# Two-layer attention and convolution encoder: four depthwise taps per layer taken out of the last two wide sections, and the last head's copy, addition and division put in another order

## The chip, the core and the metric

The kernel runs on one core of a Trainium2 chip. A core has five engines, each with its own queue of instructions that it works off in order: TensorE (PE; matrix products, into PSUM), VectorE (DVE), ScalarE (ACT), GpSimd (POOL) and SyncE (SP; it only issues transfers here). GpSimd issues transfers too. The metric is the time of one execution on the device in microseconds, lower is better.

## The reference

One sequence of 1024 positions with 1024 channels goes through two layers. Cut to the half of a layer that the change touches:

```python
h = rmsnorm(x, g_mix[l]);  p = h @ w_in[l]              # 1024 x (384 + 256 + 32 + 1024)
c_q  = rmsnorm(p[:, :384], g_q[l]);   q  = c_q @ w_uq[l]      # 8 heads x (64 + 32 rotary)
c_kv = rmsnorm(p[:, 384:640], g_kv[l]); kv = c_kv @ w_ukv[l]  # 8 heads x (64 key + 64 value)
y_attn = softmax(q k^T / sqrt(96)) v                          # per head, blocks of 128 queries
a, gt = split(p[:, 672:]);  u = a * sigmoid(gt)               # 512 channels
u = silu(layernorm(dwconv(u, w_dw_conv[l], taps=31)))         # depthwise, along the sequence
x = x + concat(y_attn, u) @ w_o[l]
x = x + gated_conv_ffn(rmsnorm(x))                            # up, 3 taps, silu gate, down
```

All is float32. The depthwise convolution is a sum of 31 taps: `conv[c, t] += w[c, tap] * u[c, t + tap - 15]`.

## The kernel before

Channels lie on the partitions, positions along the rows; a block is a tile of 128 x 1024. Each matrix product is made of three, from high and low parts of both sides (names ending in h and l), so that the result is as exact as in float32. A layer is `project` (the products with w_in, w_uq, w_ukv), `attention` and `feed` (w_o and the ConvFFN).

**`project`** walks through a list of sections. A wide section (a0 to a3, g2, g3, kv0, kv1, q0, q1, q2) multiplies the 1024 channels of h by one tile of 128 columns of w_in; the planner counts 10.9 us for it. Behind the wide sections come four short ones for the keys (k0 to k3, 2.72 us each) and six for the queries (u0, u1, n0 to n3, 4.08 us each). A section accumulates into one PSUM tile of 128 x 1024, of which `project` has three, used in turn: u0 takes the tile of k1, u1 that of k2, n0 that of k3. A key section's tile comes free in `key` (L727 to L735): ScalarE copies it into the high part kh (L733, called `kh<-pk` in the trace), then VectorE subtracts kh from it for the low part kl (L735).

The weights come by `supply` (L861), which goes by the planner's clock. GpSimd issues a transfer of the tile into its high part (`cast_tile`, L171). Later (`complete`) ScalarE writes the negative of the high part into the low part (L175) and GpSimd issues a transfer that adds the source onto it (L176). There are eight tiles for these parts; the tiles of wu1 (the weights of n2, n3 and of the rotary part) come free when section q2, the last wide one, is done with wq2.

**The 31 taps** of the depthwise convolution are done for four groups of 128 channels, into the tiles conv_0 to conv_3, in several ways, and none takes TensorE:
- near taps: one VectorE instruction each (`conv_step`, L1790), placed by the planner in `project`;
- far taps (`tap_far`, L1793 to L1797): ScalarE multiplies the group by the tap's weight into a tile (L1796), and GpSimd issues a transfer that adds the tile to conv (L1797). They are chosen in the loop over the sections (L885 to L890): in each wide section at most `FAR_TOGETHER` = 3, of the groups whose near taps are done, one per group, from the list `away[j]` of taps that the group has left;
- late taps: what is left in `away[j]` when `project` is done. `attention` spreads them over its steps (L1711 to L1723). Most are done by `tap_late` on GpSimd (L1802: multiply; L1808: a transfer adds the product to conv). In layer 0, the first 13 that group 0 has left are instead multiplied by VectorE at the steps of `STEP_AT` and added by GpSimd's own instruction (L1806) one step later. In layer 1 there are none of that kind.

**`attention`** goes through steps n = −2 to 64: eight heads with eight tiles of 128 queries each. In step n TensorE transposes the probabilities of tile n (`pt`, copied out of PSUM by ScalarE at L1615 or VectorE at L1616) and computes the scores of tile n + 2 (`s`), ScalarE takes the exponential (`p`, L1600), and in odd steps `values` (L1621) multiplies probabilities and values into a PSUM tile o (L1639). A table `agenda[n]` holds work to be recorded at the end of step n. In it stand, among others, the late taps, the first weights of w_o (transfers of four tiles at step 50, L916; their low parts, L175, from step 55 on) and the sums for the layernorm.

When half of a head (512 queries) is done, `gather` (L1649) copies one of the two halves of o with ScalarE (L1653, `yt<-o`) and adds the other with VectorE (L1654), which frees the PSUM bank. For the last head, the sums of the exponentials are inverted (`inverse`, L1682, `rc`), brought onto all partitions by TensorE (`spread`, L1685, at L301 in the trace, `rc_71s`: it takes a PSUM bank that the addition has freed), and `divide` (L1688) multiplies; `early` (L1691) begins the products with w_o in the attention's last steps and `early_add` (L1696) adds them to the residual.

Of the kernel before, what the change touches and what calls it, by code (L numbers as in the profile page):

```python
# [74 lines left out]
KEY_AT = (4.0, -8.6)  # L75
NEAR_ORDER = (0, 1, 2, 3)
FAR_TOGETHER = 3
FAR_GAP = 8.0
NPAR = P_BF + 2 * NF
HALVES = (slice(0, 512), slice(512, T))  # L80
# [39 lines left out]
class Encoder:  # L120
# [456 lines left out]
    def project(self, l, carry):  # L577
        nc, a = self.nc, self.a
        par = self.par[l]
        clock = {"pe": 0.0, "dve": 0.0}  # L580
        taps, active, u, conv, away, far_at = [], [], {}, {}, {}, {}
# [6 lines left out]
        st = {}  # L588

        def work(until):  # L590
            while True:
                at = next((e for e in active if e[0] <= clock["dve"]), None)
                if at is None and taps and clock["dve"] + TAP <= until:
                    j, t = taps.pop(0)
                    self.conv_step(l, j, u[j], conv[j], t)
                    clock["dve"] += TAP
                    continue
                if at is None:
                    at = min(active, key=lambda e: e[0], default=None)
                    if at is None or at[0] > until:  # L600
                        return
                    clock["dve"] = max(clock["dve"], at[0])
                step = next(at[1], None)
                if step is None:
                    active.remove(at)
                else:
                    clock["dve"] += step[0]
                    at[0] = clock["dve"] + step[1]

        def launch(steps, n=-1):  # L610
            active.append([clock["pe"], steps, n])

        def finish(n):
            for e in [e for e in active if e[2] <= n]:
                for step in e[1]:
                    clock["dve"] = max(clock["dve"], e[0]) + step[0]
                    e[0] = clock["dve"] + step[1]
                active.remove(e)
# [210 lines left out]
        add = lambda name, weight, emit, evict, after=None: seq.append((name, weight, emit, evict, after))  # L829
# [24 lines left out]
        times, starts, t = {}, {}, 0.0  # L854
# [6 lines left out]
        def supply(now, turn=TURN):  # L861
            while coming and coming[0][1] <= now + LEAD:
                name, at = coming.pop(0)
                turning.append((name, at, self.cast(l, name)))
            while turning and turning[0][1] <= now + turn:
                name, at, e = turning.pop(0)
                w[name] = self.complete(*e)
# [10 lines left out]
        for n, (name, weight, emit, evict, after) in enumerate(seq):  # L878
            supply(clock["pe"])
            finish(n - 3)  # L880
            ps[name] = self.wide(f"p{name}{l}")
            emit()
            clock["pe"] += times[name]
            queue = [i for i, _ in taps]
            far = [j for j in away if clock["pe"] >= far_at[j] and  # L885
                   (j not in queue or queue.count(j) == NEAR_TAPS[l][j] and queue.index(j) > 8)]
            work(clock["pe"] - times[name] / 2)
            for j in sorted(far, key=far_at.get)[:FAR_TOGETHER if times[name] > 5.0 else 0]:
                self.tap_far(l, j, away[j].pop(0), u[j], conv[j])
                far_at[j] = clock["pe"] + FAR_GAP  # L890
            work(clock["pe"])
            if after:
                after()
            launch(evict(), n)
# [665 lines left out]
    def attention(self, l, u, conv, away, spill, keys, kvs, loaded, ahead, wo, begun):  # L1560
        nc = self.nc
# [3 lines left out]
        state, v = {}, []  # L1565
# [55 lines left out]
        def values(pair, n):  # L1621
            h, qp = divmod(pair, 4)
            st = state[h]
            e = h % 2
            gg = qp // 2
            main, aux = slice(e * 64, e * 64 + 64), slice(64 - e * 64, 128 - e * 64)
            if qp % 2 == 0:
                if gg == 0 and e == 0:
                    st["y"], st["rb"] = self.blk(f"yt{l}_{h}"), self.blk(f"rb{l}_{h}")
                elif gg == 0:  # L1630
                    st["y"], st["rb"] = state[h - 1]["y"], state[h - 1]["rb"]
                st["po"] = self.bank(f"o{l}_{h}_{gg}")
            po = st["po"]
            cs = slice(qp % 2 * 256, qp % 2 * 256 + 256)
            for g in range(2):
                pt = st["pt"].pop((qp, g)).rearrange("p k q r t -> p k (q r t)")
                for i in range(4):
                    k = 4 * g + i
                    nc.tensor.matmul(po[ROW_TILES[i % 2], cs], v[k // 2][:, k % 2, h * 64:h * 64 + 64], pt[:, i, :],  # L1639
                                     start=k < 2, stop=k > 5)  # L1640
            if qp % 2 == 0:
                return
            if n >= total:
                gather(h, gg, main, aux, n)
            else:
                m = n + (h == last)
                agenda[m].append(lambda: gather(h, gg, main, aux, m))

        def gather(h, gg, main, aux, n):  # L1649
            st = state[h]  # L1650
            y, rb, po = st["y"], st["rb"], st["po"]
            qs = HALVES[gg]
            nc.scalar.copy(out=y[main, qs], in_=po[aux, :])  # L1653
            nc.vector.tensor_tensor(out=y[main, qs], in0=po[main, :], in1=y[main, qs], op=ALU.add)  # L1654
            if h < HEADS - 2:
                if gg:
                    agenda[n + 1].append(lambda: turned(h, main, rb, y))
            elif n > total:
                divide(y[main, qs], main, h, gg)
            else:  # L1660
                agenda[n + 1].append(lambda: divide(y[main, qs], main, h, gg))
                if h == last:
                    agenda[n + 1].append(lambda: finish(last, y, 0))
# [4 lines left out]
        def turned(h, main, rb, y):  # L1668
            pr = self.bank(f"sr{l}_{h}", (64, 128))
            nc.tensor.transpose(pr, self.inverse_sums, self.ident)  # L1670
            rs = self.cp.tile([8, 128], F32, name=f"rs{l}_{h}", tag="rs", bufs=2)
            nc.vector.tensor_copy(out=rs, in_=pr[0:8, :])
            nc.sync.dma_start(out=sd[h].rearrange("(a b) -> a b", a=8), in_=rs)
            nc.sync.dma_start(out=rb[main, :], in_=sd[h:h + 1].partition_broadcast(64))
            if h % 2:
                agenda[h * 8 + 10 + Y_DELAY].append(lambda: nc.gpsimd.tensor_tensor(out=y, in0=y, in1=rb, op=ALU.mult))
                agenda[h * 8 + 10 + Y_DELAY + (Y_DELAY if h < 5 else Y_LAST)].append(
                    lambda: ys.append(self.split(y, f"ys{l}_{h}", on_pool=True)))
# [9 lines left out]
        def divide(ym, main, h, c):  # L1688
            nc.vector.tensor_tensor(out=ym, in0=inv.pop((h, c))[main, :], in1=ym, op=ALU.mult)
# [10 lines left out]
        def finish(h, y, c):  # L1700
            cs = HALVES[c]
            if c == 0:
                ys.append([self.blk(f"ys{l}_{h}{i}", F32R) for i in "hl"])
            hi, lo = (t[:, cs] for t in ys[-1])
            nc.scalar.copy(out=hi, in_=y[:, cs])
            nc.vector.scalar_tensor_tensor(out=lo, in0=y[:, cs], scalar=1.0, in1=hi.bitcast(F32), op0=ALU.mult, op1=ALU.subtract)

        ys, inv, po = [], {}, begun["po"]
        total = HEADS * 8
        agenda = defaultdict(list)  # L1710
# [4 lines left out]
        for i, (_, j, t) in enumerate(late):  # L1715
            n = LATE_FROM + int((SIDE_TIME - LATE_FROM) * sum(costs[:i]) / sum(costs))
            if kinds[i] == "step":
                m, tap = STEP_AT[l][stepped.index(i)], self.tap_late(l, j, t, u[j], conv[j], nc.vector)
# [8 lines left out]
        last = HEADS - 1  # L1727
# [11 lines left out]
        for n in range(-2, total + 1):  # L1739
            if n % 2 and n > 2:  # L1740
                values((n - 3) // 2, n)
# [8 lines left out]
            if n + 2 < total:  # L1750
                h, qt = divmod(n + 2, 8)
# [18 lines left out]
            if n == total:  # L1770
                early(1, range(3))
                values(2 * total // 4 - 1, total + 1)
# [178 lines left out]
```

## Time and profile before

| | |
|---|---|
| time, median of 3 runs | 2251.78 us (2249.91 to 2252.26) |
| the profiled execution's own time | 2249.61 us |
| its span (first to last instruction in the trace) | 2247.8 us |
| TensorE busy | 2220.4 us, 99% |
| VectorE busy | 1674.3 us, 74% |
| ScalarE busy | 1242.0 us, 55% |
| GpSimd busy | 677.4 us, 30% |
| mean granted clock of TensorE | 0.996 |

A row of a timeline reads: start in us, duration in us, engine, line of the kernel, operation, output<-inputs, shapes, count (xN), and in brackets how long the engine stood idle ahead of it and what released it. Consecutive instructions of one kind are drawn together in one row with their count; a row's start is the first one's. Layer 0's sections run to about 200 us, its attention to about 400 us; layer 1's sections run to about 1316 us and its attention to about 1520 us.

### The profile page before, as it was taken

The page shows a single profiled execution, that of the slowest core. Times are in us where ns is not written, and L with a number is a line of the kernel's source. Part 1 is how long each engine was busy: PE and PEld are TensorE (multiplying, and loading weights), DVE is VectorE, ACT ScalarE, POOL GpSimd, SP SyncE. Part 2 cuts the span into 40 slices and gives each one's busy share as a digit, 9 for nine tenths or more (in the row PEclk, how much of TensorE's full clock was granted, in tenths as well). Part 3 has the DMA queues.
Part 4 walks back from the last instruction along what each step waited for, and adds up shares of the span by engine and source line. Part 5 has one row for each costly group of instructions (what it writes and reads, how often), then busy time and mean ns, then how long its engine had stood idle before and what let it go on. Part 6 is the DMA issues. An engine that isn't in the chain of part 4 may idle for free.

```text
span 2247.8 us, 34428 instructions
## 1 busy us (share of the span) xinstructions
PE 2220.4 (99%) x12750; PEld 1781.9 (79%) x12750; DVE 1674.3 (74%) x2220; ACT 1242.0 (55%) x1896; POOL 677.4 (30%) x782
## 2 busy tenths in 40 slices
PE   9999999999999999999999899999999999999998
PEld 7887666888888888888878776668888888888887
DVE  7987877668777776876579777776797777768765
ACT  5454777447555555544523557774475555555444
POOL 1232676232333332002412224542323333320032
PEclk9999999999999999999999999999999999999999
DMA  6899998766899998935958999876669999988356
GB/s 186 166 187 276 196 199 174 195 170 128 227 275 299 272 303 207 330 109 143 210 130 168 186 271 211 189 166 178 159 155 233 297 288 278 294 211 297 101 130 166
DMA packets 196921, 469.65 MB, mean 209 GB/s; under 512 B 24113, under 2 KB 32017, under 8 KB 196753
## 3 DMA queue, kind: packets, MB, share of 16 engines
q0 software_dynamic: 97904, 217.45, 48.0%
q1 hardware_dynamic: 98272, 248.96, 33.2%
q8 instruction: 100, 1.64, 0.3%
q10 hardware_dynamic: 576, 1.05, 0.1%
q14 instruction: 69, 0.56, 0.1%
HBM read 305.35 MB, written 80.40 MB: 172 GB/s over the span
## 4 chain that ended last, share of the span: by engine, by line
PE 83%; DVE 6%; DMA 5%; issue 4%; ACT 1%; POOL 1%; POOLq 0%; ACTq 0%; SPq 0%; DVEq 0%
PE p L1144 33%; PE pd L1332 17%; PE po L955 7%; PE s L1590 6%; PE o L1639 5%; PE pa L212 3%; PE t L1613 3%; PE pg L212 2%; PE pg L574 2%; PE pn L212 1%; DMA conv<-far 1%; DVE conv L1790 1%; PE pv L1574 1%; PE pu L212 1%; PE pa L574 1%
## 5 line engine op out<-in xcount | busy, mean ns | idle before, releaser
L1144 PE MATMUL p<-b,w 128*128 128x512 f32 x3552 | 807.4, 389 | 0.3
L1144 PEld LDWEIGHTS p<-b,w 128*128 128x128 f32 x3552 | 666.0, 188 | 141.0 <-DVE w L1526 1.3
L1332 PE MATMUL pd<-ab,wd 128*128 128x512 f32 (+1 forms) x1920 | 422.3, 381 | 0.0
L1332 PEld LDWEIGHTS pd<-ab,wd 128*128 128x128 f32 x1920 | 350.8, 188 | 69.5 <-DVE ab L1526 0.4
L176 POOL DMA_DIRECT2D w<-wu x96 | 84.3, 881 | 357.5 <-ACT w L175 323.9
L1592 DVE TENSOR_REDUCE mx<-s 128x1 f32<-128x1024 f32 x128 | 156.3, 1221 | 34.9 <-PE s L1590 31.4
L1600 ACT ACTIVATE p<-s,mx 128x1024 f32<-128x1024 f32 x128 | 142.9, 1117 | 55.0 <-DVE mx L1592 52.2
L1538 DVE SCALAR_TENSOR_TENSOR o<-zg,par,o 128x1023 f32<-128x1023 f32 x88 | 112.8, 1284 | 76.3 <-ACT o L1532 75.0
L1790 DVE SCALAR_TENSOR_TENSOR conv<-gate,par,conv 128x1023 f32<-128x1023 f32 (+14 forms) x127 | 161.6, 1275 | 4.5 <-ACT conv L636 1.5
L176 POOL DMA_DIRECT2D w<-in_w_up x116 | 100.4, 866 | 200.6 <-ACT w L175 174.5
L175 ACT ACTIVATE w<-w 128x512 fp32r<-128x512 f32 x212 | 133.5, 630 | 3.0
L1524 ACT CAST ab<-ac 128x512 fp32r<-128x512 f32 x130 | 80.1, 617 | 97.6 <-DVE ac L1267 94.9
L1093 DVE TENSOR_TENSOR zg<-p,zg 128x512 f32<-128x512 f32 x88 | 60.6, 690 | 98.3 <-PE p L1144 91.6
L1639 PE MATMUL o<-pt,v 128*64 128x256 f32 x1024 | 126.9, 386 | 1.7 <-DVE pt L1616 1.1
L1616 DVE COPY pt<-t 128x512 f32<-128x512 f32 x128 | 87.8, 686 | 52.6 <-PE t L1613 51.9
L916 POOL DMA_DIRECT2D wd<-in_w_down x44 | 32.6, 744 | 308.7 <-PE pd L1332 307.9
L1538 DVE SCALAR_TENSOR_TENSOR v<-zv,par,v 128x1023 f32<-128x1023 f32 x88 | 112.5, 1281 | 10.5 <-ACT v L1532 10.4
L1524 ACT CAST w<-wu 128x512 fp32r<-128x512 f32 x84 | 51.8, 619 | 123.5 <-DVE wu L1093 121.5
L1111 ACT CAST w<-wu 128x512 fp32r<-128x512 f32 x96 | 58.9, 614 | 92.7 <-DVE wu L1093 89.0
L1639 PEld LDWEIGHTS o<-pt,v 128*64 128x64 f32 x1024 | 67.7, 136 | 52.1 <-issue 18.9
L1613 PEld LDWEIGHTS t<-ident,p 64*128 64x128 f32 x2048 | 76.8, 138 | 38.3 <-issue 27.0
L1526 DVE TENSOR_TENSOR ab<-ac,ab 128x512 fp32r<-128x512 f32 x130 | 89.4, 690 | 21.2 <-ACT ab L1524 14.1
(2123 smaller groups left out, 4315.1 us busy)
## 6 DMA issues: line engine op xcount, KB each, us to landing
w<-in_w_up POOLq DMA_DIRECT2D x232, 256.0 KB, 7.4
wu<-in_w_up SPq DMA_DIRECT2D x88, 512.0 KB, 5.2
w<-wu POOLq DMA_DIRECT2D x96, 256.0 KB, 5.8
sd<-in_w_down SPq DMA_DIRECT2D x44, 512.0 KB, 9.1
ws<-sd SPq DMA_DIRECT2D x44, 512.0 KB, 8.1
wd<-in_w_down POOLq DMA_DIRECT2D x88, 256.0 KB, 5.3
act<-v SPq DMA_DIRECT2D x36, 512.0 KB, 5.7
ac<-act SPq DMA_DIRECT2D x72, 256.0 KB, 5.8
```

Source lines behind the costliest of these rows:

```text
L176: self.nc.gpsimd.dma_start(out=lo, in_=src, accum_op=ALU.add)
L212: nc.tensor.matmul(ps[:, HALVES[c]], w, x[:, HALVES[c]], start=(k == 0 and s == 0), stop=(k == n - 1 and s == 2))
L955: self.nc.tensor.matmul(ps, p[:, sl], q[:, cs], start=(k == 0 and t == 0), stop=(k == 3 and t == 2))
L1144: nc.tensor.matmul(ps, w[p][:, k * 128:(k + 1) * 128], b[:, q], start=(i in (1, 5, 2) and k == 0 and t == 0), stop=(k == 3 and t == 2), sk ...
L1332: nc.tensor.matmul(ps[t, m][:, cs], w[i, j][p][:, m * 128:(m + 1) * 128], b[:, q, cs], start=(i in (1, 5, 2) and j == 0 and s == 0), stop= ...
L1538: self.nc.vector.scalar_tensor_tensor(out=o[:, a:b], in0=z[:, at + a:at + b], scalar=self.par[l][:, tap:tap + 1], in1=o[:, a:b], op0=ALU.m ...
L1590: nc.tensor.matmul(ps[:, cs], t[r, qs], k[r, i, :], start=s == 0, stop=s == len(passes) - 1)
L1592: nc.vector.tensor_reduce(out=mx, in_=ps, op=ALU.max, axis=AX.X, negate=True)
L1600: nc.scalar.activation(out=p, in_=ps, func=AF.Exp, bias=mx, accum_out=st["sums"][:, qt:qt + 1])
L1613: nc.tensor.transpose(t[:, i, qi, :], st["p"][2 * qp + qi][r, ks], self.ident[r, r])
L1639: nc.tensor.matmul(po[ROW_TILES[i % 2], cs], v[k // 2][:, k % 2, h * 64:h * 64 + 64], pt[:, i, :], start=k < 2, stop=k > 5)
L1790: self.nc.vector.scalar_tensor_tensor(out=y[:, lo:hi], in0=u[:, lo + s:hi + s], scalar=self.tap(l, j, t), in1=y[:, lo:hi], op0=ALU.mult, o ...
```

## The change

Two things are changed, in both layers.

First, a table `FAR_LAST` limits the far taps by section: two rather than three in q1, none rather than three in q2. The four taps per layer that are not taken there stay in `away[j]` and become late taps in the attention. In layer 0 the late taps that go through GpSimd's multiply are 38 rather than 34, and group 0's 13 stepped taps begin with tap 16 rather than tap 17.

Second, in the last head: the two parts of `gather` are recorded apart. For the first 512 queries the copy is recorded in the step in which the product ends, rather than one step later, and the addition is put at the front of the next step's list. For the second 512 queries the division is put onto the list of step n, so that it is recorded behind the two `early_add`, rather than at once.

```diff
--- before.py
+++ after.py
@@ -75,6 +75,7 @@
 KEY_AT = (4.0, -8.6)
 NEAR_ORDER = (0, 1, 2, 3)
 FAR_TOGETHER = 3
+FAR_LAST = {"q1": 2, "q2": 0}
 FAR_GAP = 8.0
 NPAR = P_BF + 2 * NF
 HALVES = (slice(0, 512), slice(512, T))
@@ -885,7 +886,7 @@
             far = [j for j in away if clock["pe"] >= far_at[j] and
                    (j not in queue or queue.count(j) == NEAR_TAPS[l][j] and queue.index(j) > 8)]
             work(clock["pe"] - times[name] / 2)
-            for j in sorted(far, key=far_at.get)[:FAR_TOGETHER if times[name] > 5.0 else 0]:
+            for j in sorted(far, key=far_at.get)[:FAR_LAST.get(name, FAR_TOGETHER) if times[name] > 5.0 else 0]:
                 self.tap_far(l, j, away[j].pop(0), u[j], conv[j])
                 far_at[j] = clock["pe"] + FAR_GAP
             work(clock["pe"])
@@ -1641,22 +1642,33 @@
             if qp % 2 == 0:
                 return
             if n >= total:
-                gather(h, gg, main, aux, n)
+                for f in gather(h, gg, main, aux, n):
+                    f()
             else:
-                m = n + (h == last)
-                agenda[m].append(lambda: gather(h, gg, main, aux, m))
+                parted(h, gg, main, aux, n)
+
+        def parted(h, gg, main, aux, n):
+            copy, add = gather(h, gg, main, aux, n + (h == last))
+            agenda[n].append(copy)
+            if h == last:
+                agenda[n + 1].insert(0, add)
+            else:
+                agenda[n].append(add)
 
         def gather(h, gg, main, aux, n):
+            y, po, qs = state[h]["y"], state[h]["po"], HALVES[gg]
+            return lambda: nc.scalar.copy(out=y[main, qs], in_=po[aux, :]), lambda: gathered(h, gg, main, aux, n, po)
+
+        def gathered(h, gg, main, aux, n, po):
             st = state[h]
-            y, rb, po = st["y"], st["rb"], st["po"]
+            y, rb = st["y"], st["rb"]
             qs = HALVES[gg]
-            nc.scalar.copy(out=y[main, qs], in_=po[aux, :])
             nc.vector.tensor_tensor(out=y[main, qs], in0=po[main, :], in1=y[main, qs], op=ALU.add)
             if h < HEADS - 2:
                 if gg:
                     agenda[n + 1].append(lambda: turned(h, main, rb, y))
             elif n > total:
-                divide(y[main, qs], main, h, gg)
+                agenda[n].append(lambda: divide(y[main, qs], main, h, gg))
             else:
                 agenda[n + 1].append(lambda: divide(y[main, qs], main, h, gg))
                 if h == last:
```

What moves is seen in the order in which the instructions stand on each engine. A number behind the name of a tile counts buffers; far_1_20 and late_1_20 are the products of group 1's tap 20, conv_1 is the sum of that group; an added transfer reads `conv<-far`.

GpSimd in layer 0, from section q1 to the key sections, before:

```order
L1797 DMA conv_2_751<-far_2_19_1143 128x1020
L1797 DMA conv_0_425<-far_0_14_1146 128x1023
L1797 DMA conv_1_570<-far_1_20_1149 128x1019
L171 DMA wu00h<-in_w_uq 128x2x384
L176 DMA wu20l<-in_w_uq 128x2x384
L1797 DMA conv_0_425<-far_0_16_1240 128x1023
L1797 DMA conv_1_570<-far_1_21_1243 128x1018
L1797 DMA conv_2_751<-far_2_20_1246 128x1019
L171 DMA wu10h<-in_w_uq 128x2x384
L176 DMA wu00l<-in_w_uq 128x2x384
L176 DMA wu10l<-in_w_uq 128x2x384
```

and now:

```order
L1809 DMA conv_2_751<-far_2_19_1143 128x1020
L1809 DMA conv_0_425<-far_0_14_1146 128x1023
L172 DMA wu00h<-in_w_uq 128x2x384
L177 DMA wu20l<-in_w_uq 128x2x384
L172 DMA wu10h<-in_w_uq 128x2x384
L177 DMA wu00l<-in_w_uq 128x2x384
L177 DMA wu10l<-in_w_uq 128x2x384
```

The far additions of q2 (0_16, 1_21, 2_20) and one of q1 (1_20) are gone, so that the high part of wu1 (wu10h) now stands right behind the low part of wu2. The other places of this engine in `project` are as they were.

GpSimd near the end of layer 0's attention, up to the first transfer of w_o, before:

```order
L1806 TENSOR_TENSOR conv_0_425<-conv_0_425,late_0_28_3882 128x1011
L1802 TENSOR_SCALAR late_1_30_3930<-gate_1_420,par_63 128x1009
L1808 DMA conv_1_570<-late_1_30_3930 128x1009
L1802 TENSOR_SCALAR late_2_30_3972<-gate_2_662,par_63 128x1009
L1808 DMA conv_2_751<-late_2_30_3972 128x1009
L1806 TENSOR_TENSOR conv_0_425<-conv_0_425,late_0_29_3970 128x1010
L1802 TENSOR_SCALAR late_0_30_4059<-gate_0_417,par_63 128x1009
L1808 DMA conv_0_425<-late_0_30_4059 128x1009
L916 DMA wo_10_4062<-in_w_o 128x512
```

and now:

```order
L1814 TENSOR_SCALAR late_0_29_3881<-gate_0_417,par_63 128x1010
L1820 DMA conv_0_425<-late_0_29_3881 128x1010
L1818 TENSOR_TENSOR conv_0_425<-conv_0_425,late_0_27_3879 128x1012
L1814 TENSOR_SCALAR late_1_30_3930<-gate_1_420,par_63 128x1009
L1820 DMA conv_1_570<-late_1_30_3930 128x1009
L1814 TENSOR_SCALAR late_2_30_3972<-gate_2_662,par_63 128x1009
L1820 DMA conv_2_751<-late_2_30_3972 128x1009
L1818 TENSOR_TENSOR conv_0_425<-conv_0_425,late_0_28_3970 128x1011
L1814 TENSOR_SCALAR late_3_30_4059<-gate_3_818,par_63 128x1009
L1820 DMA conv_3_886<-late_3_30_4059 128x1009
L917 DMA wo_10_4062<-in_w_o 128x512
```

The stepped taps of group 0 now end with 28, and tap 29 is multiplied by GpSimd and added by a transfer that stands right ahead of GpSimd's own addition of tap 27 to the same tile, conv_0. Ahead of the four transfers of w_o there are four more late taps of the multiplying kind since the attention's begin than before.

ScalarE in the last head of layer 0, from the copy pt_7_20 on, before:

```order
L1615 COPY pt_7_20_4561<-t_7_200_4543 128x8x64
L1615 COPY pt_7_21_4600<-t_7_210_4582 128x8x64
L1600 ACTIVATE p_7_7_4603,sums_7_4237<-s_7_7_4564,mx_7_7_4575 128x1024
L175 ACTIVATE wo_13_4068<-wo_13_4068 128x512
L1653 COPY yt_6_4076<-o_7_0_4436 64x512
L1615 COPY pt_7_30_4642<-t_7_300_4624 128x8x64
```

and now:

```order
L1616 COPY pt_7_20_4561<-t_7_200_4543 128x8x64
L1660 COPY yt_6_4076<-o_7_0_4436 64x512
L1616 COPY pt_7_21_4601<-t_7_210_4583 128x8x64
L1601 ACTIVATE p_7_7_4604,sums_7_4237<-s_7_7_4564,mx_7_7_4575 128x1024
L176 ACTIVATE wo_13_4068<-wo_13_4068 128x512
L1616 COPY pt_7_30_4642<-t_7_300_4624 128x8x64
```

The copy of o_7_0 stands ahead of the exponential p_7_7 and of the copy pt_7_21. The order on TensorE is as it was.

## Prediction

> **What bounds the kernel now.** The page first: TensorE is busy almost throughout, so only its waits can be had back, or a wait added to it. The share of busy time, then the waits of TensorE in order of size (line, releaser, total, times, longest).
>
> ```profile
> PE 2220.4 (99%) x12750; PEld 1781.9 (79%) x12750; DVE 1674.3 (74%) x2220; ACT 1242.0 (55%) x1896; POOL 677.4 (30%) x782
> ```
>
> ```profile
> PE pu L212 <- DVE kl L735: 13.8, 2, 8.2
> PE rc_71s L301 <- DVE yt L1654: 2.0, 2, 1.0
> ```
>
> One wait stands out: section u0, once in each layer, for the subtraction that frees its PSUM slot. The timeline of TensorE there, of both layers: the last pair of the key sections, u0's first pair, and what follows u0.
>
> ```profile
> 166.92 0.61 PE L212 MATMUL pk<-kvs_1l,wk0h 128*128 128x512 f32 x2
> ...
> 173.19 1.22 PE L212 MATMUL pu<-cqs_0h,wu20h 128*128 128x512 f32 x2 [5.66 <-DVE kl L735]
> ...
> 179.09 1.04 PE L301 MATMUL rq0s<-ident,rq0y 128*128 128x128 f32 x8
> ...
> 1279.57 0.61 PE L212 MATMUL pk<-kvs_1l,wk1h 128*128 128x512 f32 x2
> ...
> 1288.36 1.22 PE L212 MATMUL pu<-cqs_0h,wu21h 128*128 128x512 f32 x2 [8.18 <-DVE kl L735]
> ...
> 1294.74 1.03 PE L301 MATMUL rq1s<-ident,rq1y 128*128 128x128 f32 x8
> ```
>
> Who holds up the subtraction: the timelines of GpSimd, ScalarE and VectorE in layer 0, and of GpSimd and ScalarE in layer 1.
>
> ```profile
> 154.99 0.86 POOL L1797 DMA_DIRECT2D conv<-far  x1 [7.25 <-DMA conv<-far]
> ...
> 157.59 1.04 POOL L171 DMA_DIRECT2D wu10h<-in_w_uq  x1
> ...
> 170.14 0.84 ACT L175 ACTIVATE wu10l<-wu10h 128x768 fp32r<-128x768 f32 x1 [9.56 <-DMA wu10h<-in_w_uq]
> 170.89 2.82 ACT L733 CAST kh<-pk 128x1024 fp32r<-128x1024 f32 x3
> 171.91 2.36 DVE L735 TENSOR_TENSOR kl<-pk,kh 128x1024 fp32r<-128x1024 f32 x2 [7.74 <-ACT kh L733]
> ...
> 1270.06 1.88 POOL L1797 DMA_DIRECT2D conv<-far  x2 [7.24 <-ACT far L1796]
> ...
> 1273.31 0.73 POOL L171 DMA_DIRECT2D wu11h<-in_w_uq  x1 [0.34 <-issue]
> ...
> 1285.31 0.84 ACT L175 ACTIVATE wu11l<-wu11h 128x768 fp32r<-128x768 f32 x1 [9.74 <-DMA wu11h<-in_w_uq]
> ```
>
> So the wait is not VectorE's own. ScalarE, in order, stands 9.56 us (layer 1: 9.74) at the low part of wu1 for a transfer; the key copies of k1 to k3 stand behind it, the subtractions behind those, u0 behind them. The transfer itself was issued by GpSimd behind three far additions, the first of which waited 7.25 us for an earlier addition to land. How long the weight transfers take, by the DMA view of four short windows (KB each, us to landing): wu1's in both layers, then the two low parts of wq2, which GpSimd issued after waits, with no far addition right ahead.
>
> ```profile
> wu10h<-in_w_uq POOLq DMA_DIRECT2D x1, 384.0 KB, 12.5
> ...
> wu11h<-in_w_uq POOLq DMA_DIRECT2D x1, 384.0 KB, 12.0
> ...
> wq21l<-in_w_in POOLq DMA_DIRECT2D x1, 512.0 KB, 5.8
> ...
> wq20l<-in_w_in POOLq DMA_DIRECT2D x1, 512.0 KB, 7.7
> ```
>
> **Part 1: no far additions ahead of wu1.** The earliest that wu1 can be issued is the end of q2, whose weights' slot it takes. The last pair of q2 in each layer, and the chain's row for the 72 matmuls of n0 to n3, which gives the pace:
>
> ```profile
> 155.14 0.62 PE L212 MATMUL pq<-xs_7h,wq20l 128*128 128x512 f32 x2
> ...
> 1267.79 0.62 PE L212 MATMUL pq<-xs_7h,wq21l 128*128 128x512 f32 x2
> ...
> 184.23 16.32 PE pn L212 x72
> ```
>
> A pair takes 16.32/36 = 0.45 us, u0's 18 matmuls 4.08. Issue is then at 155.6 (2.0 earlier) and 1268.2 (5.1 earlier). With the 5.8 to 7.7 of wq2's rows it lands at 161.4 to 163.3 and at 1274.0 to 1275.9. It is needed early enough for the low part (0.84), one key copy (2.82/3 = 0.94) and one subtraction (2.36/2 = 1.18), 3.0 in all and some 0.3 of hand-offs, before the last key pair ends at 166.92 + 0.45 = 167.37: by 164.1. In layer 1 that is 1280.02 − 3.3 = 1276.7. Both hold, by 0.8 us at worst, so u0 starts when k3 ends. What follows u0 starts at 167.37 + 4.08 = 171.45 for 179.09, **7.64 us** earlier, and at 1280.02 + 4.08 = 1284.10 for 1294.74, **10.64 us** earlier: 18.28 together. That is more than the waits' 13.8, since u0 itself runs slow after its wait. The window of it in layer 0 (busy by engine, granted clock, DMA share, GB/s):
>
> ```profile
> 173.20:177.40 4.20, 4.20 (x11) 3.34 (x12) 3.78 (x12) 0.51 (x1) 0.00 (x0) 0.57 1.05 209
> ```
>
> The clock is 0.57 there, and u0 took 5.90 us for 4.08 (layer 1: 6.38). By "TensorE: Matmul & The Clock Gate", "Part 1: The HAM clock gate", in the Trainium skill, an idle array falls to half rate and needs about 3.4 us of work to come back, which I estimate as 1.7 lost per wait, 3.4 in all, and the sum would be 17.2. The rows give 1.8 and 2.3, so the trace agrees in kind and the rows decide the size.
>
> The ScalarE multiplies of the four taps per layer go too (off the path: it waits there). What is late next in u1 and n0 are the copies of k2 and k3, freed with the same transfer; I cost them at nothing, because ScalarE's copies follow one another in 0.94 and a short section takes 4.08.
>
> **Part 2: the last head.** The end of a layer's attention, in layer 0: VectorE's reciprocal, the addition that now goes ahead of it, and TensorE's broadcast that waits for the addition's bank.
>
> ```profile
> 391.54 0.18 DVE L1682 RECIPROCAL rc<-sums 128x4 f32<-128x4 f32 x1 [1.00 <-ACT p L1600]
> ...
> 392.66 0.69 DVE L1654 TENSOR_TENSOR yt<-o,yt 64x512 f32<-64x512 f32 x1 [0.94 <-ACT yt L1653]
> ...
> 393.41 0.65 PE L301 MATMUL rc_71s<-ident,rc 128*128 128x128 f32 x4 [1.00 <-DVE yt L1654]
> ```
>
> VectorE idles 1.00 ahead of the reciprocal, and the addition (0.69) fits into it, its copy being a step earlier. The broadcast then needs the reciprocal, ready at 391.72, and TensorE is free at 393.41 − 1.00 = 392.41: the wait goes, **1.0 per layer, 2.0**. If the early copy held ScalarE's softmax up by its own half microsecond or so, half of that would be lost: 1.0 to 2.0. The division behind the early additions I cost at nothing: it is 64 rows wide and the additions, freed sooner, hide it.
>
> **Part 3: four more late taps per layer.** GpSimd's timeline in layer 0's attention: two late taps in a row, the first addition of group 0, the casts of wo, and ScalarE at the first wo tile; then the group of those additions with its waits, and two DMA prices.
>
> ```profile
> 211.66 1.43 POOL L1802 TENSOR_SCALAR late<-gate,par 128x1018 f32<-128x1018 f32 x1
> ...
> 214.00 1.44 POOL L1802 TENSOR_SCALAR late<-gate,par 128x1017 f32<-128x1017 f32 x1
> ...
> 238.74 2.38 POOL L1806 TENSOR_TENSOR conv<-conv,late 128x1022 f32<-128x1022 f32 x1 [12.62 <-DVE late L1802]
> ...
> 358.29 2.49 POOL L916 DMA_DIRECT2D wo<-in_w_o  x4
> ...
> 370.80 0.64 ACT L175 ACTIVATE wo<-wo 128x512 fp32r<-128x512 f32 x1
> ...
> 372.08 0.59 ACT L1615 COPY pt<-t 128x512 f32<-128x512 f32 x1 [0.65 <-PE t L1613]
> ```
>
> ```profile
> L1806 POOL TENSOR_TENSOR conv<-conv,late 128x1022 f32<-128x1022 f32 (+12 forms) x13 | 33.2, 2556 | 16.9 <-DVE late L1802 16.9
> ```
>
> ```profile
> conv<-late POOLq DMA_DIRECT2D x8, 504.5 KB, 7.4
> ...
> wo<-in_w_o POOLq DMA_DIRECT2D x4, 256.0 KB, 9.1
> ```
>
> A late tap is 214.00 − 211.66 = 2.34 us of GpSimd. Of the four, one stands ahead of the first addition, where GpSimd waits 12.62; three stand behind it: 7.0. One new wait comes with them: a transfer of tap 29 into group 0 now stands right ahead of GpSimd's addition of tap 27 into the same tile, which must wait for its landing, 7.4 less the 0.6 of issue: 6.8. Given back are the rest of the additions' waits, 16.9 − 12.62 = 4.3. GpSimd comes 7.0 + 6.8 − 4.3 = 9.5 us late to the wo casts, at 367.8 for 358.29. They land with 5.8 (the wq21l row) to 9.1, at 373.6 to 376.9. ScalarE wants the first at 370.80, with the attention's copy at 372.08 behind it, which TensorE needs: 373.6 + 0.64 − 372.08 = 2.2 us late, or 5.5 at the long landing, or 0 if the new wait is short. I take **+2.2**, since the four casts stand alone then as wq2's did. In layer 1 no tap is stepped, and GpSimd waits far longer for the head it has to scale, which absorbs 4 x 2.34 = 9.4:
>
> ```profile
> 1392.74 2.37 POOL L1676 TENSOR_TENSOR yt<-yt,rb 128x1024 f32<-128x1024 f32 x1 [16.90 <-DVE pt L1616]
> ```
>
> **The sum.** −18.3 − 2.0 + 2.2 = −18.1 on the profiled execution's 2249.61 us: 2231.5. That execution lies 2.17 under the median of 2251.78, so in the median's terms **2233.7**, 0.8% less. About 0.2% (4.5 us) is what a measurement of this kernel can tell from no change.
>
> **The rivals.** *The landing stays long.* If wu1's 12.5 and 12.0 came of the weights beside it, and not of the additions ahead, only the earlier issue is gained: 2.0 + 5.1 − 2.0 for the bank's wait gone + up to 2.2 lost, net about −7 and 2244.9. For it: the low parts of two more weights are issued right behind wu1. Against: wq2's transfers are larger and landed in little more than half the time.
>
> *Nothing moves.* Some other transfer or slot holds ScalarE just as long and the stall is kept: −2.0 + 2.2, 2252. Against it: ScalarE's row names wu10h, and no addition is left ahead.
>
> *VectorE and GpSimd share a port.* The VectorE multiplies of late taps in layer 0, min/median/max in ns:
>
> ```profile
> L1802 DVE TENSOR_SCALAR late<-gate,par x13: 740/750/2341, 237.9 to 351.0; 128x1022 f32<-128x1022 f32 x1, 128x1021 f32<-128x1021 f32 x1, 128x1020 f32<-128x1020 f32 x1, 128x1019 f32<-128x1019 f32 x1
> ```
>
> One of them took 2341. With a busier GpSimd all 13 could: about 12 more at 1.6 = 19 us of VectorE, spread over a stage of 113 us, and if two thirds of that reached TensorE, some 13 of the gain would be gone: 2247. "SBUF — State Buffer", "Who interferes with whom", in the Trainium skill, has such a lock between certain VectorE operations and GpSimd's, held for a whole instruction; the 2341 row is what bears it out, and the median of 750 says it is rare.
>
> *Slower: GpSimd's lag.* If GpSimd meets more waits like the new one in layer 0's attention, each 6.8 beyond the 9.5, the wo casts push the attention's copies back one for one. The gain of 20.3 is eaten from a lag of 9.5 − 2.2 + 20.3 = 27.6, three further waits; with four (lag 36.7, loss 29.4) it is 2261. For it: its additions alternate with transfers into four tiles. Against: only one such pair is new.
>
> **How the numbers follow.** Forecast 0.72, long landing 0.10, port 0.08, nothing moves 0.06, slower 0.04. Faster by over 0.2%: 0.72 + 0.10 + 0.08 = 0.90; the same 0.06; slower 0.04. The forecast's own range: at best no loss in part 3 (2231.5, and 1 us of spread of the runs: 2230.5), at worst 5.5 there and 1.0 less in part 2 (2238). To hold 8 in 10 it reaches into the long landing and port cases: 2243.
>
> **What would show it.** Right: u0's wait gone from TensorE's waits in both layers, the wait at ScalarE's wu1 under 3 us, wu1 landing in under 8; the rc wait gone; the wo casts near 368, and a wait of some 2 us of TensorE near 374. Wrong: another releaser in u0's place, wu1 at 12 again, or new TensorE waits in layer 0's attention over 6 us.

## The result, and the profile after

The changed kernel takes 2239.28 us (median of 4 runs, 2238.03 to 2239.59), the kernel before 2251.97 (4 runs, 2249.91 to 2252.26). The ratio is 0.9945, 95% interval 0.9927 to 0.9962: 12.7 us less, where 18.1 were forecast. The profiled executions stand at 2238.03 and 2249.61, a difference of 11.58. Since the order on TensorE is the same, the two traces can be laid side by side matmul by matmul; below, "lead" is how much earlier a matmul starts after the change than before.

TensorE's waits after the change, in the order of the view:

```profile
PE t L1614 <- DVE pt L1617: 4.1, 4, 2.0
PE o L1640 <- ACT pt L1616: 3.0, 1, 3.0
...
PE o L1640 <- DVE pt L1617: 1.1, 5, 0.2
PE po L956 <- DVE yt L1701: 0.9, 1, 0.9
```

The waits of u0 and of the last head's broadcast are gone. Three others are new or longer: for VectorE's copies of the probabilities (4.1 for 1.0), for a copy of ScalarE's (3.0), and in the last products of layer 0 (0.9).

**The projection.** TensorE at u0 and behind it, in both layers, then GpSimd and ScalarE at wu1 in layer 0, and wu1's transfers in the DMA view (layer 0, layer 1):

```profile
167.33 0.62 PE L213 MATMUL pu<-cqs_0h,wu20h 128*128 128x512 f32 x2
...
171.41 1.03 PE L302 MATMUL rq0s<-ident,rq0y 128*128 128x128 f32 x8
...
1280.50 0.61 PE L213 MATMUL pu<-cqs_0h,wu21h 128*128 128x512 f32 x2
...
1284.58 1.03 PE L302 MATMUL rq1s<-ident,rq1y 128*128 128x128 f32 x8
```

```profile
147.24 1.20 POOL L172 DMA_DIRECT2D wu10h<-in_w_uq  x1
...
160.43 0.83 ACT L176 ACTIVATE wu10l<-wu10h 128x768 fp32r<-128x768 f32 x1
161.24 1.01 ACT L734 CAST kh<-pk 128x1024 fp32r<-128x1024 f32 x1
```

```profile
wu10h<-in_w_uq POOLq DMA_DIRECT2D x1, 384.0 KB, 8.0
...
wu11h<-in_w_uq POOLq DMA_DIRECT2D x1, 384.0 KB, 10.1
```

u0 follows k3 without a gap. What follows u0 is at 171.41 for 179.09 (7.68 less), and in layer 1 at 1284.58 for 1294.74, 10.16 less, with a stage that began 0.5 later: 10.69 for the section itself. ScalarE's row at wu1 has no idle time any more. wu1 is issued at 147.24, 10.3 us earlier than before.

**Layer 0's attention** gives back what layer 0's projection had gained: the lead is 7.68 at its begin and −0.54 behind the first weights of w_o. One of the places, by VectorE, GpSimd and TensorE, with the granted clock of the 3.5 us behind it; first the durations of the stepped multiplies (min/median/max in ns):

```profile
L1814 DVE TENSOR_SCALAR late<-gate,par x13: 735/752/3960, 230.2 to 348.8; 128x1023 f32<-128x1023 f32 x1, 128x1022 f32<-128x1022 f32 x1, 128x1021 f32<-128x1021 f32 x1, 128x1020 f32<-128x1020 f32 x1
```

```profile
310.49 3.96 DVE L1814 TENSOR_SCALAR late<-gate,par 128x1013 f32<-128x1013 f32 x1
```

```profile
310.11 2.71 POOL L1818 TENSOR_TENSOR conv<-conv,late 128x1015 f32<-128x1015 f32 x1
312.44 1.46 POOL L1814 TENSOR_SCALAR late<-gate,par 128x1012 f32<-128x1012 f32 x1
```

```profile
315.10 0.97 PE L1614 MATMUL t<-ident,p 64*128 64x64 f32 x14 [2.01 <-DVE pt L1617]
```

```profile
315.10:318.60 3.50, 3.50 (x27) 2.85 (x29) 2.42 (x4) 1.69 (x3) 3.46 (x2) 0.51 1.05 213
```

A multiply of 0.75 us takes 3.96: it ends at 314.45, 0.55 after GpSimd's multiply ends at 313.90 and began inside the addition that GpSimd did just before. The copy pt stands behind it, TensorE waits 2.01, and then runs at clock 0.51. Three such places cost 1.3, 3.1 (1.6 of waiting and 1.5 of slow clock) and 1.1 of the lead; one such place of the kernel before is gone (0.6): 4.9 in all. The kernel before already had three multiplies of over 2 us, and TensorE waited 0.4 behind each of the last two:

```profile
249.09 2.08 DVE L1802 TENSOR_SCALAR late<-gate,par 128x1020 f32<-128x1020 f32 x1
...
316.86 2.34 DVE L1802 TENSOR_SCALAR late<-gate,par 128x1012 f32<-128x1012 f32 x1
...
350.97 2.30 DVE L1802 TENSOR_SCALAR late<-gate,par 128x1010 f32<-128x1010 f32 x1
```

After the change four take over 2 us (2.11, 2.45, 3.96, 2.27): hardly more of them, but at places where TensorE waits longer. The other loss is at the weights of w_o, by GpSimd, ScalarE and TensorE:

```profile
354.09 2.34 POOL L1818 TENSOR_TENSOR conv<-conv,late 128x1012 f32<-128x1012 f32 x1 [8.36 <-DMA conv<-late]
...
365.46 2.49 POOL L917 DMA_DIRECT2D wo<-in_w_o  x4
```

```profile
373.44 0.63 ACT L176 ACTIVATE wo<-wo 128x512 fp32r<-128x512 f32 x1 [5.13 <-DMA wo<-in_w_o]
```

```profile
374.60 1.08 PE L1640 MATMUL o<-pt,v 128*64 128x256 f32 x8 [2.97 <-ACT pt L1616]
```

GpSimd stands 8.36 us for the landing of tap 29, the weights go out at 365.46, ScalarE waits 5.13 for them and TensorE 2.97 behind it: 3.3 of the lead. In layer 1's attention, which has no stepped taps, the four more late taps cost nothing: its lead grows by 0.2 up to the last head.

**The last head** of layer 0, by VectorE and TensorE: the reciprocal and the broadcast, then the division and the first product of the feed.

```profile
392.16 0.18 DVE L1694 RECIPROCAL rc<-sums 128x4 f32<-128x4 f32 x1 [0.27 <-ACT p L1601]
...
403.18 0.69 DVE L1701 TENSOR_TENSOR yt<-rc_71s,yt 64x512 f32<-64x512 f32 x1
```

```profile
392.97 0.65 PE L302 MATMUL rc_71s<-ident,rc 128*128 128x128 f32 x4
...
403.93 0.50 PE L956 MATMUL po<-ys_1h,wo 128*128 128x512 f32 x1 [0.94 <-DVE yt L1701]
```

The broadcast no longer waits (1.0 in layer 0, 1.1 in layer 1). But in layer 0 the product po waits 0.94 for the later division, and loses 1.1; in layer 1 it waited 0.35 before, now not at all, and gains 0.5.

### The profile page after: what moved, and what is told of

Its sections match the earlier page's. It is cut to its first block, busy times and chain, and to the rows that moved or that the text cites. A ratio compares the mean times of both kernels' runs of the same rounds, so it can differ in the third digit from the quotient of the medians.

```text
span 2236.3 us, 34462 instructions
## 1 busy us (share of the span) xinstructions
PE 2217.1 (99%) x12750; PEld 1779.8 (80%) x12750; DVE 1677.3 (75%) x2220; ACT 1233.2 (55%) x1888; POOL 687.0 (31%) x790
## 4 chain that ended last, share of the span: by engine, by line
PE 87%; DVE 3%; DMA 3%; issue 3%; POOL 2%; ACT 1%; SPq 0%; POOLq 0%; ACTq 0%; DVEq 0%
PE p L1145 33%; PE pd L1333 17%; PE po L956 7%; PE s L1591 5%; PE o L1640 4%; PE pa L213 3%; PE pq L213 3%; PE t L1614 2%; PE pkv L213 2%; PE pg L213 2%; PE pg L575 2%; PE pn L213 1%; PE pv L1575 1%; PE pk L213 1%; PE pa L575 1%
## 5 line engine op out<-in xcount | busy, mean ns | idle before, releaser
L1539 DVE SCALAR_TENSOR_TENSOR v<-zv,par,v 128x1023 f32<-128x1023 f32 x88 | 112.4, 1279 | 10.1 <-ACT v L1533 10.1
L1527 DVE TENSOR_TENSOR ab<-ac,ab 128x512 fp32r<-128x512 f32 x130 | 89.2, 688 | 22.0 <-ACT ab L1525 14.9
```

The costliest lines, as they stand in the source:

```text
L1539: self.nc.vector.scalar_tensor_tensor(out=o[:, a:b], in0=z[:, at + a:at + b], scalar=self.par[l][:, tap:tap + 1], in1=o[:, a:b], op0=ALU.m ...
```

## The experiments

The theory from here on: the projection's gain is the removal of the additions, whole; 8.2 us of it are lost in layer 0's attention to the taps that moved there, 4.9 by VectorE's multiplies that GpSimd holds up and 3.3 by GpSimd's lag at the weights of w_o; the later division costs 1.1 in layer 0. Rivals stand with each run. In each group of runs the kernel before was timed too, at 2249.93 to 2251.97 us by its median, so "gain" below is the difference from the kernel before of the same group. The changed kernel gains 12.7. The intervals of the ratios reach 2 to 4 us to either side, so a difference of a few us between two variants is told by their traces and not by their times.

**Each half of the change alone.** The far taps only:

```diff
+FAR_LAST = {"q1": 2, "q2": 0}
-[:FAR_TOGETHER if times[name] > 5.0 else 0]
+[:FAR_LAST.get(name, FAR_TOGETHER) if times[name] > 5.0 else 0]
```

> Only the table of far taps is changed; the last head is as in the kernel before. Theory: the two waits of u0 go (18.4 us by the traces of before and after), and of this 4.9 us are given back in layer 0's attention where VectorE's stepped multiplies are stretched beside GpSimd's instructions, and 3.3 us where the first weights of w_o come late: 2252 - 18.4 + 8.2 = 2242. Rival: the loss in the attention comes from the last head's new order, whose copy and division stand on the same engines: then this kernel is at 2234 to 2236.

2240.3 us (ratio 0.9958, 0.9944 to 0.9972; before 2250.77): it gains 10.5, where the theory's 2242 is a gain of 10 and the rival's 2236 one of 16. By the trace it loses the same in layer 0's attention: the lead falls from 7.73 to −0.51 there, with the last head as it was. So the loss belongs to the taps.

The last head only (`gather` in two parts and the division later, far taps as before):

> Only the last head's order is changed; far taps as in the kernel before. Theory: the broadcast's wait goes in both layers (1.0 and 1.0 to 1.2 us), the later division brings TensorE a wait of 1.1 in layer 0 and takes 0.5 in layer 1: net -1.6, 2250.4. Rival: the wait in layer 0 belongs to the late weights of w_o and not to the division; then nothing is lost here and the gain is 2.7, 2249.3.

2247.97 us (ratio 0.9990, 0.9981 to 0.9999), 2.8 less by the medians, by which the rival is the nearer one; the interval (0.2 to 4.3 us) holds both. The waits of TensorE decide it: u0's are as before, the broadcast's are gone, and

```profile
PE pu L213 <- DVE kl L736: 14.5, 2, 8.5
...
PE po L956 <- DVE yt L1701: 0.9, 1, 0.9
```

the 0.9 for the division is there although the weights of w_o are not late. The rival falls; how much the head gives by itself is settled by the traces (1.5) better than by the medians.

**The four taps not computed.** The changed kernel leaving out the four taps per layer that move:

```diff
+LEFT_OUT = (((1, 20), (0, 16), (1, 21), (2, 20)), ((2, 21), (0, 26), (1, 23), (2, 22)))
+        away = {j: [t for t in away[j] if (j, t) not in LEFT_OUT[l]] for j in away}
```

> The changed kernel with the four taps per layer that move to the attention not computed at all, so that the attention's late taps are those of the kernel before. Theory (the four taps cost the 8.2 us in layer 0's attention): TensorE keeps its 7.7 us of lead through layer 0's attention, 2239.3 - 8.2 = 2231. Rival (the loss comes from the attention's earlier start against its transfers, or from chance of where the instructions meet): the time stays at 2236 to 2240.

2230.86 us (ratio 0.9914, 0.9899 to 0.9929; before 2250.77). In layer 0's attention and last head, TensorE waits for these two, of which only the division's is new:

```profile
PE t L1615 <- DVE pt L1618: 1.0, 3, 0.4
PE po L957 <- DVE yt L1702: 0.9, 1, 0.9
```

The lead of 7.79 lasts through layer 0's attention and is 8.87 at the broadcast. So the moved taps take the whole 8.2 us there, and the earlier start costs nothing. By the times they cost less: this kernel gains 19.9 for 12.7, which is 7.2, in part since TensorE loses 1.0 at another place, in layer 0's feed (`PE p L1146`, a wait for VectorE).

**Keep the additions, but issue them behind wu1.** q2's three additions are put on a list that is worked off behind the next `supply`:

```diff
             supply(clock["pe"])
+            while held_adds:
+                held_adds.pop(0)()
...
-                self.tap_far(l, j, away[j].pop(0), u[j], conv[j])
+                add = self.tap_far(l, j, away[j].pop(0), u[j], conv[j])
+                held_adds.append(add) if name == "q2" else add()
```

> The last head's new order, and all far taps kept as in the kernel before (three in q1, three in q2), but q2's three additions are issued behind the high part of wu1 instead of ahead of it. Theory (wu1 was late because it was issued and carried behind the additions): it is issued at the end of q2, lands within 8 us in both layers, u0's waits go and no tap moves to the attention: 2252 - 18.4 - 1.6 = 2232. Rival (the additions' transfers and wu1 share the transfer engines, whichever is issued first): wu1 still takes about 12 us, only the earlier issue of 2.0 and 5.1 us is gained: about 2243.

2250.19 us (ratio 1.000, 0.9991 to 1.001): neither. In layer 0 wu1 is issued at 147.28, as in the changed kernel. u0's waits are gone in both layers, as the theory had it, and the lead is 7.6 and 10 there; but it is lost again within 40 us. The waits of TensorE, and two of the transfers in layer 0:

```profile
PE s L1598 <- DMA qr<-rc: 6.7, 3, 3.6
PE pn L213 <- issue: 2.6, 1, 2.6
PE pv L1582 <- DVE qn L776: 1.7, 2, 1.3
```

```profile
conv<-far POOLq DMA_DIRECT2D x1, 509.5 KB, 15.0
...
wu10l<-in_w_uq POOLq DMA_DIRECT2D x1, 384.0 KB, 18.3
```

The windows of 160 to 180 and 180 to 193 us of this kernel and of the changed one (the last two columns are the share of the transfer engines and GB/s):

```profile
160.00:180.00 20.00, 20.00 (x98) 16.74 (x97) 16.06 (x23) 5.44 (x7) 3.38 (x4) 1.00 1.06 232
180.00:193.00 13.00, 12.91 (x57) 10.35 (x56) 10.23 (x10) 8.29 (x8) 0.85 (x1) 1.00 1.00 336
```

```profile
160.00:180.00 20.00, 20.00 (x98) 16.72 (x97) 16.05 (x24) 6.44 (x8) 2.64 (x3) 1.00 1.02 316
180.00:193.00 13.00, 13.00 (x59) 10.76 (x58) 12.96 (x13) 9.37 (x9) 0.00 (x0) 1.00 0.67 139
```

The low part of wu1 takes 18.3 us behind the additions, and the attention's first scores wait for the moves of the rotary queries. Up to 180 us the transfer engines are full in both kernels (1.06 and 1.02); from there to 193 they are at 1.00 with the additions and at 0.67 without. So it is not their place in the queue alone: behind wu1 too, the three transfers of 0.5 MB push other transfers back, and the change gains because it takes them out.

**GpSimd against VectorE.** The 13 stepped multiplies on ScalarE:

```diff
-        eng.tensor_scalar(...)
+        if eng is self.nc.vector:
+            self.nc.scalar.activation(out=p[:, lo:hi], in_=u[:, lo + s:hi + s], func=AF.Copy, scale=self.tap(l, j, t))
+        else:
+            eng.tensor_scalar(...)
```

> The changed kernel, with the 13 stepped taps of layer 0 multiplied by ScalarE instead of VectorE; GpSimd's additions of them stay. Theory (VectorE's multiply is held while GpSimd runs instructions, up to 3.96 us for 0.75, and delays the copies of the probabilities): TensorE's four waits for the copy pt on VectorE in layer 0's attention and the slow clock behind them go, 4.9 us, if ScalarE has room for 13 x 1.1 us: 2239.3 - 4.9 = 2234. Rival (the copies are late because four more taps load the transfers or the steps generally): the waits stay and the time is 2239, or more with ScalarE later.

2237.8 us (ratio 0.9945, 0.9930 to 0.9960; before 2250.17). In t the waits for VectorE's copies are gone, and the lead is 8.05 at 319.85 of the old clock, where the changed kernel has 4.75; then it is lost at another place:

```profile
PE o L1640 <- ACT pt L1616: 2.5, 1, 2.5
PE t L1614 <- ACT pt L1616: 1.9, 1, 1.9
```

```profile
328.19 1.05 ACT L195 CAST ys_3h<-yt 128x1024 fp32r<-128x1024 f32 x1 [2.40 <-POOL yt L1688]
```

ScalarE waits 2.40 for a head that GpSimd scales behind the late taps, and TensorE behind it, at slow clock again. That is neither the theory's 2234 nor the rival's kept waits: the VectorE part of the theory holds, and the waits behind GpSimd take its gain (12.4 for 12.7).

**GpSimd's lag.** A 14th stepped tap, so that tap 29 no longer goes by a transfer ahead of GpSimd's addition (`34, 36, 46, 48` becomes `34, 36, 44, 46, 48`):

> The changed kernel with one stepped tap more in layer 0 (a 14th step at 44), so that no transfer into group 0's sum stands ahead of GpSimd's own addition to it. Theory (the 8.4 us wait for that landing is the largest part of GpSimd's lag of 14.9 at the first weights of w_o): the wait goes, the weights are issued some 8 us earlier and TensorE's 3.0 us wait for the copy behind ScalarE goes: 2239.3 - 3.3 = 2236, plus or minus what one more VectorE multiply does to the copies (up to 1.5). Rival (the lag comes from the four taps' instructions themselves): the weights are still late by 2 us or more and the time is 2238 to 2239.

2235.12 us (ratio 0.9933, 0.9918 to 0.9947; before 2250.17), a gain of 15.1 for 12.7. The weights of w_o are issued 9 us earlier, and the wait behind them is not in TensorE's list:

```profile
356.23 2.50 POOL L917 DMA_DIRECT2D wo<-in_w_o  x4
```

```profile
PE t L1614 <- DVE pt L1617: 4.3, 3, 2.5
```

The waits for VectorE stay, as expected. The first weights of w_o earlier instead (`WO_AT = 50` becomes 46):

> The changed kernel with the first weights of w_o cast at step 46 instead of 50 (and the next two at 52), so that they stand ahead of the wait and of the last late taps in GpSimd's queue. Theory (the 3.0 us wait of TensorE is for these weights): it goes, 2239.3 - 3.3 = 2236. Rival (the wait only moves: the six instructions now ahead of the late taps put the sums for the layernorm later, and the tiles that the weights take come free late): 2238 to 2241.

2233.56 us (ratio 0.9927, 0.9912 to 0.9941; runs of 2231.84 to 2236.44): ScalarE finds the weights there, its wait is gone, and so is TensorE's. The gain is 16.6 for 12.7: 3.9, where 3.3 were forecast. The profiled run is the fastest of the four, and in it VectorE's part is 2.2 us instead of 4.1; how much is lost to held multiplies differs from kernel to kernel, with where they meet.

**The division.** Layer 0 divides ahead of the early additions, layer 1 behind them:

```diff
-                agenda[n].append(lambda: divide(y[main, qs], main, h, gg))
+                f = lambda: divide(y[main, qs], main, h, gg)
+                agenda[n].append(f) if l else f()
```

> The changed kernel with the second division of layer 0 put back ahead of the early additions; layer 1 as changed. Theory (TensorE's first product po in layer 0 takes the bank that the division reads, so the later division makes it wait 0.94): that wait goes, 2239.3 - 1.1 = 2238.2. Rival (the wait is for the early additions or the layernorm's sums as well): it stays under another name, 2239.

2240.07 us (ratio 0.9955, 0.9938 to 0.9971; runs of 2236.93 to 2240.19), a gain of 10.1. Inconclusive by the time. In the trace the wait of po is gone, and nothing of the lead is lost between the broadcast and the feed, where the changed kernel loses 1.1.

**Both repairs**, the weights at 46 and the division:

> Both repairs together: the first weights of w_o at step 46, and layer 0's second division ahead of the early additions. Theory: the earlier weights gave 5.7 us by the medians (2233.6), the division another 1.1: 2232.5. Rival (the division moves nothing that the rest of layer 0 does not wait for anyway): 2233.5.

2231.74 us (5 runs, 2231.43 to 2234.22; ratio 0.9920, 0.9906 to 0.9933; before 2249.93), a gain of 18.2 for the 16.6 of the weights alone. That does not tell the theory from the rival. In the trace po's wait is gone, but VectorE's held multiplies make TensorE wait 3.9 in t for 2.2, and both profiled spans are 2230.0. With q1's third far tap kept as well (`{"q2": 0}`):

> Both repairs, and q1 keeps its three far taps, so that three taps per layer move instead of four. Theory (what held wu1 was q2's additions alone, the first of them waiting in GpSimd's queue; q1's third is issued before them): u0's waits stay gone in both layers, GpSimd has 2.34 us less in each attention: 2231 to 2232.5. Rival (q1's third addition is part of the hold-up): wu1 lands later, u0 waits again for up to a few us: 2234 to 2240.

2231.96 us (ratio 0.9915, 0.9901 to 0.9928), a gain of 18.0; u0's waits stay gone. The cut in q1 was not needed. And with no stepped tap at all in layer 0 (`STEP_AT = ((), ())`):

> Both repairs, and in layer 0 no stepped taps: all of group 0's late taps are multiplied by GpSimd and added by transfers, as in layer 1. Theory (VectorE's stepped multiplies are what GpSimd holds up): TensorE's waits for the copy pt on VectorE, 2.2 us in the kernel with the early weights, go, and GpSimd's own time stays (13 x 2.34 for 13 x 2.4): 2230.5 to 2231.5. Rival (13 more transfers of 0.5 MB in a stage whose transfer engines are busy 0.94 of the time): GpSimd waits for landings, and the weights of w_o or the queries come late: 2236 or more.

2242.05 us (ratio 0.9961, 0.9948 to 0.9975). No copy of VectorE's is waited for in t any more, and GpSimd's lag becomes the bound, by its waits from 200 to 370 us and by ScalarE:

```profile
POOL conv L1821 <- DMA conv<-late: 41.2, 14, 7.6
```

```profile
337.10 1.04 ACT L195 CAST ys_3h<-yt 128x1024 fp32r<-128x1024 f32 x1 [9.44 <-POOL yt L1689]
```

```profile
PE t L1614 <- ACT pt L1616: 10.7, 2, 9.0
```

The rival is right there: the added transfers make GpSimd wait for landings, and a single wait of ScalarE for GpSimd costs TensorE 9.0.

## Why the prediction came out as it did, point by point

- *u0's wait goes, 7.64 and 10.64 us, with the slow clock.* Right: 7.68 and 10.69 of lead, and u0 at full clock in 4.08 us in both layers (171.41 − 167.33, 1284.58 − 1280.50). By the prediction's estimate from "TensorE: Matmul & The Clock Gate", "Part 1: The HAM clock gate", in the Trainium skill, it would have been 17.2; measured were 18.4.
- *wu1 can be issued at the end of q2 at the earliest, and lands in 5.8 to 7.7.* Wrong, without consequence: it goes out at 147.24, while q2's products run to 155.6, so the tile that it takes is not wq2's, as the section on the kernel has it, but one that is free earlier. In the kernel before, the three additions held it in GpSimd's queue for 10.3 us and not for 2.0, most of it the first one's wait of 7.25 for a landing. In layer 1 it goes out 11.3 us earlier, counted from the section's begin, and there the row of the first names ScalarE's multiply. The landing took 8.0 and 10.1. In layer 0 it landed at 155.2, 9 us ahead of the time by which it was needed. The rival of the long landing was thus no rival: with 12.5 us of landing from 147.24 it would have been there at 159.7 too.
- *The additions merely stand in the way.* Incomplete, as the held additions show: they also load the transfer engines just where the queries' moves run. The forecast spoke of the queue alone. The kernel that keeps them behind wu1 was expected at 2232 by its steps and takes 2250.
- *The last head, −2.0.* The broadcast is right (−1.0 and −1.1); the division, put at nothing, is +1.1 in layer 0 and −0.5 in layer 1: −1.5 together. The step that failed is that the additions hide it: in layer 0, it stands on the path of the first product po itself.
- *Four more late taps, +2.2.* This is the term that was mis-sized: 8.2 by the traces, 7.2 by the gain of the kernel without these taps. GpSimd's lag from its first addition to the weights of w_o was put at 9.5 and is 14.9 (134.4 us from 231.06 to 365.46, for 119.55 from 238.74 to 358.29): the new wait was 8.4 for 6.8, and its other waits shrank by 0.9 (15.1 to 14.2) and not by 4.3. At TensorE this is 3.3. The larger part, 4.9, is the multiplies of VectorE: the rival of the shared port was the right mechanism at the wrong size. All 13 were priced at 13 us; in fact some are held, for up to 3.2 us each, and three of them reach TensorE. It should have stood in the sum, and "rare" misread its row, which gives only the shortest, the median and the longest: three of the 13 took over 2 us before, and TensorE already waited behind two of them. "SBUF — State Buffer", "Who interferes with whom", in the Trainium skill, says that the one which issues first holds the port for its whole instruction. The trace agrees on the hold: each held multiply ends about 0.55 after one of GpSimd's ends. Which was first it does not show: by their rows, three of the four over 2 us begin 0.13 to 0.44 ahead of that multiply of GpSimd's, while GpSimd is issuing a transfer.
- *Sum.* −18.4 − 1.5 + 8.2 = −11.7 for the measured −11.58 of the profiled executions. The forecast's own worst case was 2238; the measured 2239.3 lies beyond it, within the room up to 2243 that was left for the rivals. Part 1 came out to 0.1 although its time of issue was 8.4 us off: that was luck, covered by the 9 us in hand.

## What to carry to other kernels

When work is moved off a crowded stretch, look where it lands as closely as at where it leaves: here the stretch gave all of 18.4 us, and the place that took the work, an engine 30% busy, took 8.2 back through two engines that only meet it now and then. An engine far from its bound can still be late: what counts is the longest chain of waits in its queue ahead of something that is needed (the weights of w_o). Casting these four steps earlier removed the wait for them and raised the gain from 12.7 to 16.6. A transfer can hold up others twice, in the queue in which it waits and on the engines that carry it; changing the order cures only the first.

## What the runs showed of the hardware that was not expected

Short waits are enough for the slow clock, but not always: behind 2.01 us at 315.10 TensorE ran at 0.51 for 3.5 us and lost 1.5, behind 2.97 at 374.60 it ran at 1.00 and lost nothing more in that profile, and in the kernel with ScalarE's multiplies 2.5 us at the same place were followed by a clock of 0.55, which lost 1.6. "TensorE: Matmul & The Clock Gate", "Part 1: The HAM clock gate", in the Trainium skill, has a window that runs free of the kernel, which fits that equal waits cost unequally; these runs don't show the window itself.
